# Layer norm of a convolution module: sums about the mean of six of eight feature tiles, made during the convolution's last groups, and two first maps of the second product in step

## The chip, the cores and the metric

The kernel runs on one core of one Trainium2 chip. The metric is the device time of one execution in microseconds; the time of a kernel is the median of its runs. The engines are named as in the profile: PE multiplies matrices (its weight loads are shown as PEld), DVE, ACT and POOL work on vectors, and DMA queues move data. Each engine takes its instructions in their order and stops at one whose operands or whose output buffer are not ready.

## What is computed

A trunk of two layers works on 1024 latent tokens and 256 context tokens of 1024 features. The first layer's mixer is a convolution module, the second's is attention; a feed-forward network (FFN) follows each. The change lies in the convolution module alone, between its convolution and its second product (`w_pw2`):

```python
def layernorm(x, g, b):
    xf = x.astype(jnp.float32)
    mu = jnp.mean(xf, axis=-1, keepdims=True)
    var = jnp.mean(jnp.square(xf - mu), axis=-1, keepdims=True)
    y = (xf - mu) * lax.rsqrt(var + EPS)
    return (y * g.astype(jnp.float32) + b.astype(jnp.float32)).astype(x.dtype)

def conv_module(h, w_pw1, b_pw1, w_dw, b_dw, ln_g, ln_b, w_pw2, b_pw2):
    u = h @ w_pw1 + b_pw1
    a, gt = jnp.split(u, 2, axis=-1)
    u = a * jax.nn.sigmoid(gt)
    u = lax.conv_general_dilated(u, w_dw[:, None, :].astype(u.dtype), ...) + b_dw
    u = jax.nn.silu(layernorm(u, ln_g, ln_b))
    return u @ w_pw2 + b_pw2
...
    yx = conv_module(hx, *cp)
    yc = conv_module(hc, *cp) if need_ctx else None
...
    x = x + g_x * rmsnorm(yx, norm_g[i, 1])
    ctx = ctx + g_c * rmsnorm(yc, norm_g[i, 1])
    fx = rmsnorm(x, norm_g[i, 2]) * (1.0 + scf_x) + shf_x
    x = x + gf_x * rmsnorm(swiglu(fx, ffn_w1[i], ffn_w3[i], ffn_w2[i]), norm_g[i, 3])
```

## The kernel before

**Layout.** Features lie on the 128 partitions, so 1024 features are eight feature tiles (KT = 8), and tokens run along the columns. Behind the convolution the tokens are three pieces: C (256 context tokens), L and R (512 latent tokens each).

**Convolution.** It has 64 groups: eight feature tiles of eight groups each (`conv`). A group is a run of matmuls (L497 and its neighbours) of weight maps, which DVE makes with one product each (L468), two for a group. The group's result in PSUM is drained by ACT with the bias (L498) into a buffer v, and DVE adds the second half to it (L500). In v the tokens of a feature tile stand in another layout, so a finished feature tile is stored to DRAM and loaded back token by token in order: `load_cv` (L537) brings it into the tensors of C, L and R (tags KB, T4, T5). The eighth tile of C goes from v to its tensor by eight DMAs, which ACT issues (L505). DVE sums each feature tile in v for the mean (`conv_sum`, L520 and L522), the eighth in two halves.

**Layer norm.** `ln` takes one piece: `mean` makes the mean of all its tokens on all partitions by matmuls with a constant (L530); for each of the eight tiles DVE subtracts it (L548), ACT squares (L351, L354) and DVE adds up (L355). `stat` sums over the partitions with matmuls of one column (L331), DVE scales them (L336) and takes the reciprocal root in eleven small operations (`rsqrt`, L309 to L317), and PE transposes it so that it stands on all partitions (L343). Then for each tile DVE multiplies by root and gain (L556), ACT does Silu with the bias (L558), and the result is split in a high half (ACT, L153) and a low half (DVE, L156).

**Products.** A product of float32 operands is three matmuls of such halves (`mm3`, L164 to L166: high by high, high by low, low by high). `pw2` makes eight maps of a piece, each of 8 x 3 matmuls over the eight tiles, with weights from `wload`: a DMA of 512 KB (L140), the high half on ACT (L141), the low half on DVE (L145). Two raw buffers (`wr`) and three buffers of each half (`wh`, `wl`) go round. ACT evacuates a map from PSUM (L572) and squares it for the sum that the RMS norm behind needs. `post_pre` does that norm, adds the residual (L592, L595), and makes the FFN's input (`apply`, L363 to L369).

**Order.** The program's text calls: normalise C, normalise L, maps of C, normalise R, maps of L, `post_pre` of C and L, maps of R, then the FFN of layer 0 over C and L, with R's `post_pre` beside it. A scheduler of the tile framework places instructions on each engine from that text by priorities (`later` puts an instruction further back). The first two weights of `pw2` are loaded during the convolution's last groups. PSUM has eight banks; the convolution goes round three (3, 4 and 7), maps and statistics have sets of banks that `set_banks` names.

## Time and profile before

| | |
|---|---|
| median of 3 runs | 3082.22 us (3081.51, 3082.22, 3088.68) |
| the profiled execution's own time | 3085.12 us |
| span of the profiled execution | 3083.3 us |
| busy in the span: PE | 2918.8 us (95%) |
| DVE | 1913.3 us (62%) |
| ACT | 1192.3 us (39%) |
| POOL | 259.8 us (8%) |

All durations below are of that one profiled execution. Times in the trace count from the span's start. The convolution ends near 392 us, the FFN's first matmul starts near 554 us; the stretch between them is the place of the change. A row of the trace shows the start, the busy time, the engine, the kernel's line, the operation, its output and its inputs with their shapes, the number of records in the row, and in brackets the idle time of the engine ahead of it with what ended that. PEclk is the clock that the chip granted to PE, as a share of full speed. Where a table row has a count but no time, it groups all instructions of one line.

### The profile page before, as it was taken

Reading aid. Unit: us, or ns where it says so; the run is one execution under the profiler, and the core shown is the slowest. Engines: PE = TensorE matmul, PEld = TensorE weight load, DVE = VectorE, ACT = ScalarE, POOL = GpSimd, SP = SyncE. Lnnn points to the kernel's source line nnn. Section 1 sums busy time; section 2 is a strip of 40 time slices with the busy share of each in tenths; the row PEclk is TensorE's granted clock in tenths of the full one; section 3 lists DMA queues with packets and bytes.
Section 4 is the critical chain, followed back from the end, with each engine's and each line's share of the span. In section 5 each row is a group of like instructions: output and inputs, shape, how many; then the busy total and the mean of one; then the engine's idle time right before and its main releaser. Section 6 shows DMA issues by size and latency. Waiting matters only on the chain. (4 is left out here: it accounts for less than half of the span.)

```text
span 3083.3 us, 38930 instructions
## 1 busy us (share of the span) xinstructions
PE 2918.8 (95%) x14974; PEld 2427.3 (79%) x14974; DVE 1913.3 (62%) x3355; ACT 1192.3 (39%) x1869; POOL 259.8 (8%) x413
## 2 busy tenths in 40 slices
PE   7999969998999999999988899979999999999997
PEld 5788858887888888888876678767777778788886
DVE  5886777897533257433574899776666653843335
ACT  5222255431211234222332688655555543332222
POOL 0000001123100011000013211110000000100000
PEclk9999979999999999999988999989999999999999
DMA  6542424466422234333355321222222232442232
GB/s 234 149 119 75 129 85 138 149 189 222 150 63 68 62 99 155 109 96 96 115 155 125 87 61 43 87 78 81 67 81 76 67 127 96 150 136 96 92 95 68
DMA packets 140714, 336.94 MB, mean 109 GB/s; under 512 B 39920, under 2 KB 61424, under 8 KB 139376
## 3 DMA queue, kind: packets, MB, share of 16 engines
q1 hardware_dynamic: 76432, 221.94, 22.3%
q0 software_dynamic: 37984, 104.42, 11.5%
q10 hardware_dynamic: 26112, 8.10, 1.1%
q8 instruction: 117, 1.92, 0.3%
q14 instruction: 69, 0.57, 0.1%
HBM read 289.76 MB, written 39.19 MB: 107 GB/s over the span
## 5 line engine op out<-in xcount | busy, mean ns | idle before, releaser
L164 PE MATMUL ps<-T,wh 128*128 128x512 f32 (+1 forms) x2256 | 852.9, 379 | 14.4 <-ACT T L153 5.5
L166 PE MATMUL ps<-T,wl 128*128 128x512 f32 (+1 forms) x2256 | 850.3, 378 | 15.6 <-DVE wl L145 15.6
L165 PE MATMUL ps<-T,wh 128*128 128x512 f32 (+1 forms) x2192 | 824.8, 377 | 1.0 <-DVE T L156 0.7
L141 ACT CAST wh<-wr 128x1024 fp32r<-128x1024 f32 x296 | 310.8, 1050 | 895.4 <-PE ps L165 672.5
L145 DVE TENSOR_TENSOR wl<-wr,wh 128x1024 fp32r<-128x1024 f32 x288 | 352.3, 1224 | 314.6 <-ACT wh L141 310.9
L166 PEld LDWEIGHTS ps<-T,wl 128*128 128x128 f32 x2256 | 431.8, 191 | 94.7 <-DVE wl L145 18.2
L164 PEld LDWEIGHTS ps<-T,wh 128*128 128x128 f32 x2256 | 431.4, 192 | 93.7 <-ACT T L153 7.0
L165 PEld LDWEIGHTS ps<-T,wh 128*128 128x128 f32 x2192 | 419.6, 191 | 74.8 <-DVE T L156 2.0
L165 PE MATMUL ps<-HS,wh 128*128 128x512 f32 (+1 forms) x784 | 304.2, 388 | 0.0
L853 DVE TENSOR_TENSOR T<-ps,T 128x512 fp32r<-128x512 f32 x320 | 216.9, 687 | 110.8 <-ACT T L852 109.7
L166 PE MATMUL ps<-HS,wl 128*128 128x512 f32 (+1 forms) x720 | 279.4, 388 | 0.0
L164 PE MATMUL ps<-HS,wh 128*128 128x512 f32 (+1 forms) x720 | 279.3, 390 | 0.0
L852 ACT CAST T<-ps 128x512 fp32r<-128x512 f32 x320 | 185.9, 585 | 191.7 <-PE ps L849 165.4
L849 PE MATMUL ps<-cst,T 128*128 128x128 f32 x1100 | 192.1, 276 | 15.5 <-DVE T L853 15.3
L681 DVE TENSOR_TENSOR T<-ps,T 128x512 f32<-128x512 f32 (+1 forms) x168 | 110.7, 664 | 146.3 <-PE ps L166 145.5
L837 DVE TENSOR_SCALAR_CACHE_REDUCE T<-ps,rq 128x1280 f32<-128x1280 f32 x110 | 170.0, 1545 | 42.0 <-PE ps L831 37.7
L849 PEld LDWEIGHTS ps<-cst,T 128*128 128x128 f32 x1100 | 133.5, 142 | 63.3 <-DVE T L853 43.5
L657 DVE TENSOR_TENSOR sm<-sm,ps 128x256 f32<-128x256 f32 (+1 forms) x88 | 54.6, 620 | 197.8 <-PE ps L166 197.8
L839 ACT ACTIVATE T<-T,mn 128x1280 f32<-128x1280 f32 x110 | 150.3, 1367 | 67.7 <-DVE T L837 65.8
L165 PEld LDWEIGHTS ps<-HS,wh 128*128 128x128 f32 x784 | 147.9, 189 | 28.8 <-DVE HS L156 0.2
L831 PE MATMUL ps<-KB,q 128*128 128x512 f32 (+1 forms) x576 | 143.5, 369 | 16.7 <-DVE T L837 8.2
L166 PEld LDWEIGHTS ps<-HS,wl 128*128 128x128 f32 x720 | 135.8, 189 | 27.0
(212 smaller groups left out, 4331.9 us busy)
## 6 DMA issues: line engine op xcount, KB each, us to landing
wr<-in_w SPq DMA_DIRECT2D x220, 512.0 KB, 3.5
q<-in_w SPq DMA_DIRECT2D x44, 512.0 KB, 3.5
wr<-in_pw SPq DMA_DIRECT2D x40, 512.0 KB, 3.6
q<-in_wmodT POOLq DMA_DIRECT2D x56, 256.0 KB, 3.4
HR<-in_wmodT POOLq DMA_DIRECT2D x56, 256.0 KB, 3.4
qsd<-T POOLq DMA_DIRECT2D x32, 256.0 KB, 10.9
q<-qsd POOLq DMA_DIRECT2D x32, 256.0 KB, 3.3
wr<-in_wo SPq DMA_DIRECT2D x16, 512.0 KB, 3.8
```

What stands on the lines that cost most here:

```text
L141: nc.scalar.copy(hi, raw)
L145: nc.vector.tensor_tensor(lo, raw, hi.bitcast(F32), op=ALU.subtract)
L164: nc.tensor.matmul(out[:, :n], lhsT=wh, rhs=xh, start=k == 0, stop=False)
L165: nc.tensor.matmul(out[:, :n], lhsT=wh, rhs=xl, start=False, stop=False)
L166: nc.tensor.matmul(out[:, :n], lhsT=wl, rhs=xh, start=False, stop=k == nk - 1)
L681: nc.vector.tensor_tensor(yd, out[:, :c1 - c0], yd, op=ALU.add)
L831: nc.tensor.matmul(sc[:, k0:k0 + w], lhsT=q[:, h, :], rhs=kt[:, p * TOK + k0:p * TOK + k0 + w], start=p == 0, stop=p == 1)
L837: nc.vector.tensor_scalar(out=pt, in0=sc, scalar1=rq[:, h:h + 1], scalar2=None, op0=ALU.mult, op1=ALU.min, accum_out=mn)
L839: nc.scalar.activation(pt, pt, AF.Exp, bias=mn, scale=-1.0, accum_out=sums[:, 0, h:h + 1])
L849: nc.tensor.transpose(tp[:, h * P:(h + 1) * P], Ps[h][:, j * P:(j + 1) * P], c["ident"])
L852: nc.scalar.copy(ph, tp)
L853: nc.vector.tensor_tensor(pl, tp, ph.bitcast(F32), op=ALU.subtract)
```

## The change

Normalising no longer starts from the mean of all eight feature tiles. `conv_sum` runs over the first six tiles only (KM = 6), and their mean, on three banks of its own for C, L and R (`ln_mean`), is subtracted as a shift. A variance about a shift needs two sums, of the values and of their squares: variance is the mean square less the square of the mean, both taken about the shift. `ln_tile` does for one tile and one piece the subtraction on DVE (now with a factor, so another form of operation), the square on ACT, and the sums over the partitions as one-column matmuls on PE (placed `later(100)`): for C both sums of each tile, for L and R the sum of the values of each tile, while their squares are added up on DVE as before and summed at the end. The first seven tiles of C and L are taken three at a time behind the convolution's groups from the seventh of the groups left in that loop on (`i > 5`); their eighth tiles and all of R stand behind the convolution.

`ln` then makes two numbers for each token, the reciprocal root and the mean by the root. Both are transposed to all partitions (two banks), and a tile is normalised by two operations of DVE (multiply, subtract) where there was one; the gain moves to the scale operand of ACT's Silu. In `pw2` the first two maps of each piece run in step (`projs`, `mm3s`): for each of the eight input tiles three matmuls of map 0 and three of map 1. The eight DMAs of C's eighth tile are issued by SP where ACT issued them. The banks are dealt out anew: sums of C and of R share bank 5, the maps have banks 7, 1, 6, the statistics behind them 3 and 4.

In the order of PE's instructions, the first place is behind the convolution's last group. In these rows `ps` is a PSUM bank, HS and T_2697 the convolution's data and maps, HR its sums, cst a constant, acc the summed squares, nr the reciprocal root, and T_3214 with wh the first map of C. Before:

```order
L497 MATMUL ps<-HS,T_2697 128x324
L530 MATMUL ps<-HR,cst 128x32 x8
L331 MATMUL ps<-cst,acc 128x1 x2
L343 MATMUL ps<-cst,nr 128x128 x2
L164 MATMUL ps<-T_3214,wh 128x256 x3
L165 MATMUL ps<-T_3214,wh 128x256
```

In the changed kernel PE has these rows there; KB, T_3011 and T_3019 are the tensors of C, L and R, sb the squares of a C tile, ne the mean by the root, and L176 is a product of C:

```order
L515 MATMUL ps<-HS,T_2697 128x324
L567 MATMUL ps<-cst,KB 128x1 x2
L567 MATMUL ps<-cst,sb 128x1 x2
...
L567 MATMUL ps<-cst,T_3011 128x1 x28
L567 MATMUL ps<-cst,KB 128x1 x2
L567 MATMUL ps<-cst,sb 128x1 x2
L567 MATMUL ps<-cst,T_3019 128x1 x28
L596 MATMUL ps<-cst,nr 128x128 x2
L567 MATMUL ps<-cst,T_3011 128x1 x4
L596 MATMUL ps<-cst,ne 128x128 x2
L567 MATMUL ps<-cst,T_3019 128x1 x4
L567 MATMUL ps<-cst,acc 128x1 x4
L176 MATMUL ps<-T_3310,wh 128x256 x2
```

Sums of L and of seven tiles of R now stand on PE between C's sums and C's transposes, and the eighth tiles' sums between the transposes and C's first product.

The second place is on DVE, where R is normalised beside the first maps of L. HS is R's normalised low half, T_3655 or T_3774 its high half, `wr` and `wl` the raw and low half of a weight. Before, the splits of the weights of maps 0 to 3 of L stand further ahead, and that of map 4 is the one in these rows:

```order
L556 SCALAR_TENSOR_TENSOR T_3022<-T_3022,cst,ps 128x512 x5
L156 TENSOR_TENSOR HS<-T_3022,T_3655 128x512 x2
...
L556 SCALAR_TENSOR_TENSOR T_3022<-T_3022,cst,ps 128x512
L156 TENSOR_TENSOR HS<-T_3022,T_3655 128x512 x2
L145 TENSOR_TENSOR wl<-wr_74,wh 128x1024
L156 TENSOR_TENSOR HS<-T_3022,T_3655 128x512 x2
```

In the changed kernel it is the split of map 3 of L, and it is behind 23 of the 24 operations of R:

```order
L602 TENSOR_TENSOR T_3019<-T_3019,ps 128x512 x2
L603 TENSOR_TENSOR T_3019<-T_3019,ps 128x512 x2
...
L603 TENSOR_TENSOR T_3019<-T_3019,ps 128x512
L157 TENSOR_TENSOR HS<-T_3019,T_3774 128x512
L373 TENSOR_TENSOR acc<-acc,sb 128x512
L146 TENSOR_TENSOR wl<-wr_73,wh 128x1024
L157 TENSOR_TENSOR HS<-T_3019,T_3774 128x512
```

The split of a weight has moved back by one map against the normalisation of R. The same holds, still on DVE, beside the last maps of R, where L's residual is added (L592 and L595 before, L642 and L645 after; T_3689 and T_3816 are L's tensor, HR the residual). Before, the split ahead of that is that of R's map 6:

```order
L145 TENSOR_TENSOR wl<-wr_74,wh 128x1024
L592 SCALAR_TENSOR_TENSOR T_3689<-T_3689,col_2944,ps 128x512 x2
L595 TENSOR_TENSOR T_3689<-T_3689,HR 128x512 x2
...
L595 TENSOR_TENSOR T_3689<-T_3689,HR 128x512 x2
L145 TENSOR_TENSOR wl<-wr_73,wh 128x1024
```

In the changed kernel the split of map 6 stands behind all sixteen operations:

```order
L642 SCALAR_TENSOR_TENSOR T_3816<-T_3816,col_2944,ps 128x512 x2
L645 TENSOR_TENSOR T_3816<-T_3816,HR 128x512 x2
...
L645 TENSOR_TENSOR T_3816<-T_3816,HR 128x512 x2
L146 TENSOR_TENSOR wl<-wr_74,wh 128x1024
```

The split for map 6 has gone from the row ahead of L's residual to the row behind it, where map 7's was. The diff:

```diff
--- before.py
+++ after.py
@@ -38,6 +38,7 @@
 NM = 5
 CG = 8
 NC_, NL = CTX // PH, SEQ // PH
+KM = KT - 2
 UW = 2 + NC_ + 2 + NL + 2
 OW = UW - 4
 PIECES = {"C": (0, CTX), "L": (CTX, CTX + 512), "R": (CTX + 512, TOK)}
@@ -164,6 +165,23 @@
             nc.tensor.matmul(out[:, :n], lhsT=wh, rhs=xh, start=k == 0, stop=False)
             nc.tensor.matmul(out[:, :n], lhsT=wh, rhs=xl, start=False, stop=False)
             nc.tensor.matmul(out[:, :n], lhsT=wl, rhs=xh, start=False, stop=k == nk - 1)
+
+    def mm3s(self, outs, ws, x, nk, n):
+
+        nc = self.nc
+        for k in range(nk):
+            xh, xl = x(k)
+            for out, w in zip(outs, ws):
+                wh, wl = w(k)
+                nc.tensor.matmul(out[:, :n], lhsT=wh, rhs=xh, start=k == 0, stop=False)
+                nc.tensor.matmul(out[:, :n], lhsT=wh, rhs=xl, start=False, stop=False)
+                nc.tensor.matmul(out[:, :n], lhsT=wl, rhs=xh, start=False, stop=k == nk - 1)
+
+    def projs(self, outs, waps, x, n):
+        def cols(w):
+            return lambda k: (w[0][:, k * P:(k + 1) * P], w[1][:, k * P:(k + 1) * P])
+        ws = [cols(self.pre.pop(0) if self.pre else self.wload(w)) for w in waps]
+        self.mm3s(outs, ws, x, KT, n)
 
     def proj(self, out, wap, x, n):
         hi, lo = self.pre.pop(0) if self.pre else self.wload(wap)
@@ -502,16 +520,15 @@
                 for d, o0, nn in ((self.vc, 0, NC_), (self.vl, 2 + NC_, NL)):
                     if k == KT - 1 and d is self.vc:
                         for j in range(CG):
-                            nc.scalar.dma_start(self.cvs["C"][16 * j:16 * j + 16, k, :], v[:, j, :NC_])
+                            nc.sync.dma_start(self.cvs["C"][16 * j:16 * j + 16, k, :], v[:, j, :NC_])
                     else:
                         nc.scalar.dma_start(d[k].rearrange("g q n -> q g n"), v[:, :, o0:o0 + nn])
                 if k == KT - 1:
                     self.load_cv("L", k)
                     self.load_cv("R", k)
 
-                self.conv_sum(v[:, CG // 2:] if k == KT - 1 else v, k)
-            elif k == KT - 1 and g == CG // 2 - 1:
-                self.conv_sum(v[:, :CG // 2], k)
+                if k < KM:
+                    self.conv_sum(v, k)
             yield
 
     def conv_sum(self, v, k):
@@ -521,41 +538,70 @@
         if k:
             nc.vector.tensor_tensor(self.vsum, self.vsum, r, op=ALU.add)
 
-    def mean(self, b):
-
-        nc = self.nc
-        ps = self.bank("st")
+    def ln_mean(self, b, ps):
+
+        nc = self.nc
         nn, o, s0 = {"C": (NC_, 0, 0), "L": (NL, 2 + NC_, 0), "R": (NL, 2 + NC_, 4)}[b]
         for i in range(PH if b == "C" else 4):
             nc.tensor.matmul(ps[:, i * nn:(i + 1) * nn], lhsT=self.c["selp"][:, s0 + i:s0 + i + 1].to_broadcast([P, P]),
                              rhs=self.vsum[:, o:o + nn], start=True, stop=True)
-        return ps
+
+    def ln_tile(self, b, k, mean, sums):
+
+        nc = self.nc
+        n = PIECES[b][1] - PIECES[b][0]
+        x, J = self.cvs[b][:, k, :], n // P
+        nc.vector.scalar_tensor_tensor(out=x, in0=mean[:, :n], scalar=-float(KT) / KM, in1=x, op0=ALU.mult, op1=ALU.add)
+        if b == "C":
+            sq = self.sb(n)
+            nc.scalar.activation(sq, x, AF.Square)
+            vs = (x, sq)
+        else:
+            if k == 0:
+                self.lnacc[b] = self.acc(n)
+            self.sq_acc(self.lnacc[b], x, k)
+            vs = (x, self.lnacc[b]) if k == KT - 1 else (x,)
+        with self.later(100):
+            for i, v in enumerate(vs):
+                for j in range(J):
+                    nc.tensor.matmul(sums[:, i * J + j:i * J + j + 1], lhsT=v[:, j * P:(j + 1) * P], rhs=self.c["ones"],
+                                     start=k + i + j == 0, stop=k == KT - 1 and i == 1 and j == J - 1)
 
     def load_cv(self, b, k):
         d = (self.vc if b == "C" else self.vl)[k].rearrange("g (c s) n -> (g c) (s n)", s=PH)
         n = PIECES[b][1] - PIECES[b][0]
         self.nc.sync.dma_start(self.cvs[b][:, k, :], d[:, 512:] if b == "R" else d[:, :n])
 
-    def ln(self, b, stags, box):
+    def ln(self, b, stags, box, mean, sums, bcast):
 
         nc, c = self.nc, self.c
         c0, c1 = PIECES[b]
         n = c1 - c0
+        J = n // P
         cv = self.cvs[b]
-        mean = self.mean(b)[:, :n]
-        acc = self.acc(n)
-        for k in range(KT):
-            nc.vector.tensor_tensor(cv[:, k, :], cv[:, k, :], mean, op=ALU.subtract)
-            self.sq_acc(acc, cv[:, k, :], k)
+        for k in range(KT if b == "R" else 0):
+            self.ln_tile(b, k, mean, sums)
             yield
-        pb = self.stat(acc, n)
+
+        m, q, e = (self.tiny([P, 16], t) for t in ("nv", "nd", "ne"))
+        d, v = m[:, :J], m[:, J:2 * J]
+        nc.vector.tensor_scalar(out=m[:, :2 * J], in0=sums[:, :2 * J], scalar1=1.0 / D, scalar2=None, op0=ALU.mult)
+        nc.vector.tensor_tensor(q[:, :J], d, d, op=ALU.mult)
+        nc.vector.scalar_tensor_tensor(out=v, in0=v, scalar=EPS, in1=q[:, :J], op0=ALU.add, op1=ALU.subtract)
+        r = self.rsqrt(v, J)
+        nc.vector.tensor_tensor(e[:, :J], d, r, op=ALU.mult)
+        for ps, t in zip(bcast, (r, e)):
+            for j in range(J):
+                with self.later(16):
+                    nc.tensor.transpose(ps[:, j * P:(j + 1) * P], t[:, j:j + 1].to_broadcast([P, P]), c["ident"])
+        pr, pd = (ps[:, :n] for ps in bcast)
         shi, slo = self.halves(*stags, n)
         box.append((shi, slo))
         for k in range(KT):
             z = cv[:, k, :]
-            nc.vector.scalar_tensor_tensor(out=z, in0=z, scalar=c["lng"][:, k:k + 1], in1=pb,
-                                           op0=ALU.mult, op1=ALU.mult)
-            nc.scalar.activation(z, z, AF.Silu, bias=c["lnb"][:, k:k + 1], scale=1.0)
+            nc.vector.tensor_tensor(z, z, pr, op=ALU.mult)
+            nc.vector.tensor_tensor(z, z, pd, op=ALU.subtract)
+            nc.scalar.activation(z, z, AF.Silu, bias=c["lnb"][:, k:k + 1], scale=c["lng"][:, k:k + 1])
             self.split(shi[:, k, :], slo[:, k, :], z)
             yield
 
@@ -567,8 +613,12 @@
         yacc = self.acc(n)
         box.append((y, yacc))
         for k in range(KT):
-            o = self.bank("mm")
-            self.proj(o, self.a["pw2"][k], self.pairs(*s), n)
+            if k == 0:
+                os = [self.bank("mm") for _ in range(2)]
+                self.projs(os, self.a["pw2"][0:2], self.pairs(*s), n)
+            o = os[k] if k < 2 else self.bank("mm")
+            if k > 1:
+                self.proj(o, self.a["pw2"][k], self.pairs(*s), n)
             nc.scalar.activation(y[:, k, :], o[:, :n], AF.Identity, bias=c["bpw2"][:, k:k + 1], scale=1.0)
             self.sq_acc(yacc, y[:, k, :], k)
             yield 24 * n / 2400
@@ -998,23 +1048,37 @@
         for g0 in (0, CG // 2):
             self.split_u(KT - 1, g0, g0 + CG // 2)
         self.derive(0, (1, 2))
+        bk = [self.ps[:, i, :] for i in range(8)]
+        shift = {"C": bk[0], "L": bk[1], "R": bk[2]}
+        sums = {"C": bk[5], "L": bk[6], "R": bk[5]}
+        bcast = {"C": (bk[0][:, :CTX], bk[0][:, CTX:]), "L": (bk[3], bk[4]), "R": (bk[2], bk[0])}
+        self.lnacc = {}
+        early = [(b, k) for b in ("C", "L") for k in range(KT - 1)]
         for i, _ in enumerate(cg):
             if i in (2, 4):
                 self.pre.append(self.wload(a["pw2"][i // 2 - 1]))
-        self.set_banks(mm=[0, 1, 2, 3, 4, 7], st=[5, 6])
+            if i == 5:
+                for b in PIECES:
+                    self.ln_mean(b, shift[b])
+            for _ in range(3 if i > 5 else 0):
+                if early:
+                    b, k = early.pop(0)
+                    self.ln_tile(b, k, shift[b], sums[b])
         sv, yv, fv = ({b: [] for b in PIECES} for _ in range(3))
         tags = {"C": ("KB", ("T1", "T1"), ("T1", "T1")), "L": ("T4", ("T2", "T3"), ("T2", "T3")),
                 "R": ("T5", ("T6", "HS"), ("T4", "T6"))}
 
         def pp(b):
             return self.post_pre(0, *yv[b][0], a["xT"], self.x1d, *PIECES[b], 0, "HR", tags[b][2], fv[b])
+        self.set_banks(mm=[7, 1, 6], st=[3, 4])
         for b in ("C", "L"):
-            for _ in self.ln(b, tags[b][1], sv[b]):
+            self.ln_tile(b, KT - 1, shift[b], sums[b])
+        for b in ("C", "L"):
+            for _ in self.ln(b, tags[b][1], sv[b], shift[b], sums[b], bcast[b]):
                 pass
-            self.bank("st")
         for _ in self.pw2("C", tags["C"][0], sv["C"][0], yv["C"]):
             pass
-        for _ in self.ln("R", tags["R"][1], sv["R"]):
+        for _ in self.ln("R", tags["R"][1], sv["R"], shift["R"], sums["R"], bcast["R"]):
             pass
         for _ in self.pw2("L", tags["L"][0], sv["L"][0], yv["L"]):
             pass
```

## The prediction

> **What bounds the kernel now.** I read the windows of the convolution's end first, then the rows of PE, DVE and ACT there. C, L and R are the three token pieces (256, 512, 512 columns); m0 to m7, L0 to L7 and R0 to R7 are their eight maps of the second product.
>
> ```profile
> core 0: us, PE busy (x) PEld busy (x) DVE busy (x) ACT busy (x) POOL busy (x), PEclk, DMA share, GB/s
> 391.00:410.00 19.00, 5.72 (x25) 4.87 (x24) 11.38 (x37) 6.44 (x15) 0.00 (x0) 0.57 0.19 58
> 430.00:444.80 14.80, 7.80 (x55) 7.11 (x53) 13.51 (x27) 12.71 (x23) 0.00 (x0) 0.77 0.23 73
> 457.30:482.00 24.70, 24.70 (x105) 20.41 (x106) 20.71 (x39) 15.81 (x26) 0.00 (x0) 0.91 0.28 88
> 482.00:504.00 22.00, 22.00 (x102) 18.26 (x100) 10.10 (x11) 11.56 (x17) 0.00 (x0) 1.00 0.43 141
> ```
>
> Between the convolution and L0, PE is mostly idle and DVE or ACT is late; from 457.3 us PE is full. So an edit ahead of 457 us is worth what it does to the start of that full stretch, and a hole made in the stretch costs its full length. The last row holds L4 to L7: 22.0 / 4 = 5.5 us a map, 0.227 us a matmul. PE's rows with their waits:
>
> ```profile
> 379.79 0.34 PE L497 MATMUL ps<-HS,T 128*128 128x324 f32 x1
> ...
> 389.62 0.35 PE L497 MATMUL ps<-HS,T 128*128 128x324 f32 x1
> ...
> 390.92 0.35 PE L497 MATMUL ps<-HS,T 128*128 128x324 f32 x1
> 394.75 3.62 PE L530 MATMUL ps<-HR,cst 128*128 128x32 f32 x16 [3.48 <-DVE HR L522]
> 403.94 1.02 PE L331 MATMUL ps<-cst,acc 128*128 128x1 f32 x4 [5.57 <-DVE acc L355]
> 407.38 0.69 PE L343 MATMUL ps<-cst,nr 128*128 128x128 f32 x2 [2.42 <-DVE nr L317]
> 409.87 1.01 PE L164 MATMUL ps<-T,wh 128*128 128x256 f32 x3 [1.81 <-ACT T L153]
> ...
> 416.16 0.28 PE L165 MATMUL ps<-T,wh 128*128 128x256 f32 x1
> 416.28 0.28 PE L166 MATMUL ps<-T,wl 128*128 128x256 f32 x1
> ...
> 426.70 0.95 PE L331 MATMUL ps<-cst,acc 128*128 128x1 f32 x8
> ...
> 442.47 2.08 PE L530 MATMUL ps<-HR,cst 128*128 128x128 f32 x8 [6.75 <-DVE T L556]
> ...
> 454.09 0.50 PE L164 MATMUL ps<-T,wh 128*128 128x512 f32 x1 [1.52 <-ACT wh L141]
> ...
> 457.29 0.80 PE L166 MATMUL ps<-T,wl 128*128 128x512 f32 x1 [2.47 <-DVE wl L145]
> ...
> 547.88 0.50 PE L166 MATMUL ps<-T,wl 128*128 128x512 f32 x1 [1.29 <-DVE wl L145]
> ...
> 562.21 1.01 PE L164 MATMUL ps<-T,wh 128*128 128x512 f32 x2 [4.00 <-ACT T L368]
> ```
>
> C's statistics (two sums, two transposes) cost PE little, and its first map starts at 409.87. A C matmul takes 0.12 us (416.16 to 416.28, 2.9 us a map). Two later stops carry my argument: at 457.29 PE waits for the low half of L0's weights, split on DVE; at 562.21 it waits for L's input to the FFN. DVE's rows:
>
> ```profile
> 378.19 0.32 DVE L500 TENSOR_TENSOR HR<-HR,ps 128x162 f32<-128x162 f32 x1
> 378.43 0.82 DVE L468 TENSOR_TENSOR T<-q,cst 128x640 fp32r<-128x640 f32 x1
> 379.16 2.49 DVE L520 TENSOR_REDUCE sm<-HR 128x162 f32<-128x1296 f32 x1
> ...
> 398.41 1.42 DVE L548 TENSOR_TENSOR KB<-KB,ps 128x256 f32<-128x256 f32 x4 [3.71 <-PE ps L530]
> ...
> 433.26 2.06 DVE L556 SCALAR_TENSOR_TENSOR T<-T,cst,ps 128x512 f32<-128x512 f32 x3
> ...
> 443.53 1.22 DVE L145 TENSOR_TENSOR wl<-wr,wh 128x1024 fp32r<-128x1024 f32 x1
> ...
> 446.74 3.08 DVE L548 TENSOR_TENSOR T<-T,ps 128x512 f32<-128x512 f32 x5
> ...
> 456.02 1.22 DVE L145 TENSOR_TENSOR wl<-wr,wh 128x1024 fp32r<-128x1024 f32 x1
> ...
> 470.47 3.38 DVE L556 SCALAR_TENSOR_TENSOR T<-T,cst,ps 128x512 f32<-128x512 f32 x5 [1.21 <-PE ps L343]
> ...
> 479.51 1.22 DVE L145 TENSOR_TENSOR wl<-wr,wh 128x1024 fp32r<-128x1024 f32 x1
> ...
> 559.52 1.23 DVE L145 TENSOR_TENSOR wl<-wr,wh 128x1024 fp32r<-128x1024 f32 x1 [4.64 <-ACT wh L141]
> 560.66 2.06 DVE L363 SCALAR_TENSOR_TENSOR sb<-T,col,ps 128x512 f32<-128x512 f32 x3
> ```
>
> DVE takes its queue in order, so a split behind a normalisation waits for it: m6's (443.53) behind L's, which began at 433.26; L4's (479.51) inside R's (from 470.47), where it hurt nothing because L1 to L3 were split already. From these rows, a two-input operation costs 0.60 us at 512 columns (3.08 for five) and 0.34 at 256 (1.42 for four), a drain of a convolution group 0.24 and a map product 0.73 (378.19 to 379.16). A split takes 1.22, 1.13 before the next operation can follow. PE's rows give the reciprocal root: 2.4 from the sums' end at 404.96 to the transposes at 407.38.
>
> **The change, step by step.**
>
> *Convolution's end.* The reduction of the seventh tile (2.49) and the two halves of the eighth, as wide together, leave DVE: with three adds, some 5.8 us. In their place, ahead of the last five drains, stand seven subtractions each of C, L and R: 7 x 0.34 + 14 x 0.60 = 10.8 us. Their form has no row of that kind here; the nearest are L651 (below: constant scalar, 0.68 us) and L556 (column scalar, 2.06 for three). So 0.60 to 0.66 each; I take 0.60, by the constant scalar. The three means (32 records) run on PE behind the group that ended at 380.1 (379.79), 3.9 us at full clock; then five groups of 1.30 (389.62 to 390.92), with 24 records of sums between them, end at 393.5. DVE: five map products and three drains from 378.43 end at 382.8; 10.8 us of subtractions and five drains more, at 394.8, against 393.05. Eight DMAs leave ACT for SP. They made ACT's step:
>
> ```profile
> 390.91 0.40 ACT L498 ACTIVATE HR<-ps,cst 128x162 f32<-128x162 f32 x1 [0.99 <-DVE HR L500]
> 391.70 0.55 ACTq L505 DMA_DIRECT2D KB<-HR  x1
> 392.30 0.40 ACT L498 ACTIVATE HR<-ps,cst 128x162 f32<-128x162 f32 x1 [0.99 <-DVE HR L500]
> ...
> 435.89 1.33 ACT L558 ACTIVATE T<-T,cst 128x512 f32<-128x512 f32 x2
> 437.13 1.12 ACT L153 CAST T<-T 128x512 fp32r<-128x512 f32 x2
> ...
> 454.76 2.69 ACT L354 ACTIVATE sb<-T 128x512 f32<-128x512 f32 x5
> L651 DVE SCALAR_TENSOR_TENSOR sm<-sm,ps 128x512 f32<-128x512 f32 x22 | 14.9, 680 | 0.0
> wr<-in_pw SPq DMA_DIRECT2D x40, 512.0 KB, 3.6
> ```
>
> That step (1.39 us a group, 390.91 to 392.30) goes, but DVE is now the late one, so I count nothing for it. On SP only loads that wait for the same drains stand behind them.
>
> *One-column sums.* Before, C, L and R need 10 such matmuls, now 104, each of two records with a weight load apiece. Eight records took 0.95 us at full clock (426.70), 0.12 each; four took 1.02 at the low clock (403.94), 0.25 each. PE has just run the convolution, so I take 0.12. The order shows that L's 28 do not lie beside the convolution: they and four more C tiles stand behind its last group (393.5): 32 records to 397.3, L's 56 to 404.0, C's last 8 to 405.0. R's 56 use C's bank, so they wait until DVE has read it (405.2) and end at 412.0; only then come C's transposes, though the root is ready at 407.6. Before: 407.38.
>
> Then DVE's second entry is L's statistic, which waits for 24 more records and ne's transposes (415.6). C's first normalised tile is done at 416.3, its first product at 417.9, **8 us later** than 409.87.
>
> The Trainium skill, "TensorE: Matmul & The Clock Gate", Part 1, says that about 3.4 us of sustained activity gives the full clock and an idle window of that length takes it back. By it the sums run at full clock behind the convolution, and the sum below stays +10.5. Part 4 of that page says that transposes do not count as busy in the same way; if that held of one-column work too, the sum would be +23. Here 16 small records in 3.62 us (394.75) did not raise the clock, and no row has a long run of them at full clock, so the trace settles neither.
>
> *C and L normalised.* The factor moves to ACT's operand for nothing; DVE takes two operations where one was: C costs 24 x 0.34 + 2 of roots = 10 us, from 415.7 to 425.8. m0 to m2 have weights and end at 430.2. m3's split stands behind 22 of L's 24 operations, 13.2 us from 426.3, and 0.7 of waiting for ACT, which has two weight casts and two evacuations first: 440.2, done 441.4. Before, m6 was at that point at 444.75. What hid the change's gain: R's mean no longer stops PE (6.75 us at 442.47), but the same L operations now hold m3. Five maps at 2.9, with about 2 us lost to the low clock after the idle, end at 457.6. So L0's third matmul comes at 458.0, against 457.29: **+0.8**.
>
> *L in step, R's normalisation.* L0 and L1 together take 48 x 0.227 = 10.9, with R's sums and eight transposes 13.3, to 470.9. Three weight buffers exist, and L2's split is done (464). L3's stands in DVE's queue behind R's normalisation, which can begin only after those transposes (469.7). It comes after 23 operations of 0.60 and an add, 14.4 us, and ACT, with L3's and L4's casts and the evacuations first and 1.13 a tile (0.62 + 0.51, above), stretches it to 485.6. PE has L2 alone to hide it, and arrives at 476.8: **idle 8.8 us**. It resumes at the low clock, as at 457.29: there the window of 24.7 us had 0.91 of the clock, 9% or 2.2 us lost. I add 2.2. L3 ends at 493.1; before at 482, where the window of L4 begins. **+11**.
>
> *To the FFN.* L4 to L7 have their splits in time: 514.9. R0 and R1 take 10.9, R2 to R5 5.5 each, sums and transposes 2.7: 550.5. R6's split stands behind L's post (from 541.2; 8 x 0.66 + 14 x 0.60 = 13.7 us), so R6 waits from 551.0 to 556.1 and is slow again; before, R7 lost 1.29 there. R6 ends at 563.2. L's second statistic stands behind nine matmuls of R7 (2.0); its sums take 1.0, the root with a split in it 3.3, transposes 0.4: L's input starts on DVE at 569.9, against 560.66: **+9.2**. In exchange, the split that stood ahead of that (559.52, after 4.64 idle) now stands behind it, for the product that follows: +1 to +2. The rest of the program has the same order, and the FFN is full of PE.
>
> **Sum: +10.5 us.** The profiled run took 3085.1 us (span 3083.3, 1.8 around it), 2.9 above the median 3082.2. So 3095.6 against itself, 3092.7 against the median.
>
> Bounds: a first part 5 us quicker or R6's wait gone gives +5; both, +0.5. Subtractions at 0.66 add 0.8; a weight load that lands in 6 instead of 3.6 us adds up to 2; sums at 0.25 add 12 to 14, that is +23.
>
> **Rivals.**
>
> *The lateness is absorbed (not slower).* PE's end before was loose by 4.0 at 562.21 and 1.29 at 547.88. If R's normalisation hides behind L2 because ACT's casts come earlier, and R6 behind R5, only the first part counts: +0.8 less those 5.3, so -4.5, about 3078. It decides when L3's and R6's waits together stay under 5.3 us. For it: DVE was only 10.1 of 22 us busy at 482 to 504. Against it: both splits stand in order behind work that begins too late, 14.4 and 13.7 us for 5.5 of cover.
>
> *Sums at the low clock.* Some 100 of the records between 393.5 and 415 at 0.25 instead of 0.12 move C's start by 12 to 13 us, and all behind it: 3105. For it: 394.75, where the clock stayed low. Against it: 426.70, eight such records at full clock amid other work.
>
> *The early work comes through (faster).* If the sums run between convolution groups in spite of their order, C starts at 410 as before, 8 us earlier than in my sum, and with both waits hidden as in the first rival that gives 0.8 - 8 - 5.3 = -12.5: 3070. Against it is the order, which an engine does not pass.
>
> **How the numbers follow.** My forecast (+4 to +16 us, 3086 to 3098) has 0.6, absorbed 0.23, low clock 0.1, faster 0.07. The range, 3077 to 3103, leaves out the last two and little of the others. A measurement tells 0.3% (9.2 us) from no change. Of the forecast's 0.6, 0.38 lies above that bound: with the low clock 0.48 slower. Its other 0.22 and 0.21 of the absorbed case are within: 0.43. The rest, 0.02 and 0.07, is faster: 0.09.
>
> **What would show it.** Right: C's transposes about 412; the first product about 418; a wait of PE for a DVE split of 8 to 9 us near 477 and of about 5 near 551; the FFN's L part some 9 to 12 us late. Wrong: C's product before 413, sums at 0.25, or no stop of PE between L0 and L7.

## The result, and the profile after

The changed kernel takes 3118.01 us (median of 4 runs, 3113.43 to 3127.42) and the kernel before, in its four runs beside it, 3085.45 us (3081.51 to 3093.88). The ratio is 1.0099, with a 95% interval of 1.0078 to 1.0121: it is slower by about 1%, 30 us, three times the forecast and outside its range. The profiled execution took 3118.28 us (span 3116.5), 33.2 us more than that of before.

The windows of the changed kernel at the convolution's end, in the columns that were used above (PE, PEld, DVE, ACT, POOL, then PEclk):

```profile
380.00:388.00 8.00, 8.00 (x68) 8.00 (x67) 8.00 (x19) 3.49 (x10) 1.24 (x2) 1.00 0.77 224
388.00:392.00 4.00, 4.00 (x37) 4.00 (x35) 4.00 (x9) 1.23 (x3) 0.00 (x0) 1.00 0.11 18
392.00:400.00 8.00, 8.00 (x39) 8.00 (x39) 4.73 (x9) 2.70 (x5) 0.00 (x0) 0.50 0.03 4
400.00:426.00 26.00, 25.75 (x122) 25.66 (x122) 6.59 (x23) 4.00 (x6) 2.83 (x4) 0.50 0.26 82
426.00:434.00 8.00, 5.88 (x29) 5.80 (x29) 2.50 (x10) 1.36 (x3) 0.00 (x0) 0.50 0.00 0
```

PE is busy almost without a pause from 380 to 426 us, and yet the granted clock falls to 0.50 at 392 and stays there up to 434. What it is busy with, from the timeline of PE with its waits:

```profile
379.89 3.73 PE L546 MATMUL ps<-HR,cst 128*128 128x32 f32 x32
...
388.70 0.50 PE L567 MATMUL ps<-cst,KB 128*128 128x1 f32 x4
...
399.97 12.09 PE L567 MATMUL ps<-cst,T 128*128 128x1 f32 x56
...
414.02 12.11 PE L567 MATMUL ps<-cst,T 128*128 128x1 f32 x56 [0.25 <-DVE nv L588]
425.99 0.67 PE L596 MATMUL ps<-cst,nr 128*128 128x128 f32 x2
...
434.18 0.80 PE L176 MATMUL ps<-T,wh 128*128 128x256 f32 x2 [2.30 <-ACT T L154]
...
458.72 0.58 PE L167 MATMUL ps<-T,wl 128*128 128x256 f32 x1 [11.35 <-DVE wl L146]
...
503.38 0.79 PE L167 MATMUL ps<-T,wl 128*128 128x512 f32 x1 [7.96 <-DVE wl L146]
...
576.14 0.67 PE L167 MATMUL ps<-T,wl 128*128 128x512 f32 x1 [4.67 <-DVE wl L146]
```

The one-column sums are L567. At first four records take 0.50 us (388.70), 0.12 each, later 56 take 12.1, 0.21 each. C's first product starts at 434.18 us, where it was 409.87 before. Behind it stand the three waits for a weight's low half that the prediction named: m3's (458.72), L3's (503.38) and R6's (576.14). On DVE, L3's split and L's input to the FFN:

```profile
501.51 0.68 DVE L373 TENSOR_TENSOR acc<-acc,sb 128x512 f32<-128x512 f32 x1
502.11 1.22 DVE L146 TENSOR_TENSOR wl<-wr,wh 128x1024 fp32r<-128x1024 f32 x1
...
585.51 2.06 DVE L381 SCALAR_TENSOR_TENSOR sb<-T,col,ps 128x512 f32<-128x512 f32 x3 [1.77 <-PE ps L361]
```

### The profile page after: what moved, and what is told of

Read it like the earlier page. It is cut to its first block, busy times and chain, and to the rows that moved or that the text cites. A ratio compares the mean times of both kernels' runs of the same rounds, so it can differ in the third digit from the quotient of the medians.

```text
span 3116.5 us, 39346 instructions
## 1 busy us (share of the span) xinstructions
PE 2954.4 (95%) x15172; PEld 2466.2 (79%) x15172; DVE 1918.9 (62%) x3375; ACT 1196.7 (38%) x1869; POOL 260.3 (8%) x413
## 3 DMA queue, kind: packets, MB, share of 16 engines
q10 hardware_dynamic: 24960, 7.96, 1.1%
## 5 line engine op out<-in xcount | busy, mean ns | idle before, releaser
L167 PE MATMUL ps<-T,wl 128*128 128x512 f32 (+1 forms) x2208 | 832.6, 378 | 33.6 <-DVE wl L146 33.6
L165 PE MATMUL ps<-T,wh 128*128 128x512 f32 (+1 forms) x2208 | 835.1, 379 | 6.7 <-ACT T L154 3.9
L166 PE MATMUL ps<-T,wh 128*128 128x512 f32 (+1 forms) x2160 | 812.3, 376 | 0.6 <-DVE T L387 0.4
L167 PEld LDWEIGHTS ps<-T,wl 128*128 128x128 f32 x2208 | 422.0, 191 | 110.3 <-DVE wl L146 35.6
L165 PEld LDWEIGHTS ps<-T,wh 128*128 128x128 f32 x2208 | 422.2, 191 | 83.1 <-ACT T L154 5.0
L166 PEld LDWEIGHTS ps<-T,wh 128*128 128x128 f32 x2160 | 412.3, 191 | 72.8 <-DVE T L157 1.2
```

The lines of the kernel that those rows point to most:

```text
L165: nc.tensor.matmul(out[:, :n], lhsT=wh, rhs=xh, start=k == 0, stop=False)
L166: nc.tensor.matmul(out[:, :n], lhsT=wh, rhs=xl, start=False, stop=False)
L167: nc.tensor.matmul(out[:, :n], lhsT=wl, rhs=xh, start=False, stop=k == nk - 1)
```

## The experiments

Times moved a little from one set of runs to the next (the kernel before had medians of 3085.45 to 3088.98), so each kernel is compared by its ratio to the kernel before in the same set; 0.001 is 3.1 us, and what a version gains or loses is worked out from the ratios. The changed kernel's own ratio is 1.0099.

### Are the sums slow because they move one column?

Each sum is made with 32 equal columns, same weights, same count:

```diff
-nc.tensor.matmul(sums[:, i * J + j:i * J + j + 1], lhsT=v[:, j * P:(j + 1) * P], rhs=self.c["ones"],
+o = (i * J + j) * 32
+nc.tensor.matmul(sums[:, o:o + 32], lhsT=v[:, j * P:(j + 1) * P], rhs=self.c["ones"].to_broadcast([P, 32]),
...
-in0=sums[:, :2 * J]
+in0=sums[:, :2 * J * 32].rearrange("p (a w) -> p a w", w=32)[:, :, 0]
```

> The changed kernel, with each one-column sum (128x1) made as the same matmul with 32 equal columns (128x32), so the same weights and the same count of records. Theory clock: a long run of one-column matmuls does not hold PE's clock, and the trace's 0.50 of the clock from 400 to 434 us comes from them; the means with 32 columns (3.73 us for 32 records, at 379.89) ran at the full clock, so 32 columns hold it. Then a record takes 0.12 and not 0.21 us, C's first product comes near 418 to 420 instead of 434.18 us, and the time falls by 13 to 17 us, to 3101 to 3105. Theory other cause: the clock falls there whatever the sums do (the end of the convolution alone, or the weight load of each record). Then the records stay at 0.21 us, the clock at 0.50 to 0.55 from 400 to 426 us, and the time stays at 3115 to 3121.

Measured: 1.0098 (1.0076 to 1.0119), the time of the other cause. The clock did not hold. But it fell at 395.2 us, later than with one column, and with one column it had fallen at 392.0, ahead of the convolution's last matmul (392.94): both speak against the convolution's end as the cause. (The 391.2 in the next expectation is too early; from 391 to 392 us the clock of the changed kernel was still 0.99.) So the same edit was run with 64 columns:

> The changed kernel with 64 equal columns in each sum (32 columns did not hold the clock: it fell at 395.2 us, four microseconds later than with one column, 391.2). Theory columns: what holds the clock is how many columns stream in a given time; 64 columns stream twice as many, so the clock falls later still or not at all, and C's first product comes at 418 to 427 us; the time is 3102 to 3112. Rival, the convolution's end: the clock falls 3 to 4 us after the last convolution matmul whatever small matmuls follow; then it falls at 395 to 397 us, C's first product comes at 430 us and the time is as with 32 columns, 3114 to 3120.

Measured: 1.0031 (1.0021 to 1.0040), 21 us less than the changed kernel, and less than the first theory had named. Windows with 32 columns, then with 64:

```profile
392.00:396.00 4.00, 4.00 (x35) 4.00 (x34) 3.74 (x8) 2.36 (x5) 0.00 (x0) 0.90 0.05 8
396.00:426.00 30.00, 29.75 (x141) 29.61 (x141) 7.33 (x25) 4.00 (x6) 2.84 (x4) 0.50 0.22 71
```

```profile
392.00:400.00 8.00, 8.00 (x73) 8.00 (x73) 6.76 (x13) 4.68 (x9) 0.70 (x1) 1.00 0.30 77
400.00:414.00 14.00, 13.12 (x116) 12.85 (x116) 7.24 (x30) 3.78 (x7) 2.13 (x4) 1.00 0.32 110
```

PE's timeline with 64 columns (the sums are L568 here):

```profile
396.01 6.42 PE L568 MATMUL ps<-cst,T 128*128 128x64 f32 x56
...
407.65 0.38 PE L597 MATMUL ps<-cst,nr 128*128 128x128 f32 x2
...
413.68 0.50 PE L176 MATMUL ps<-T,wh 128*128 128x256 f32 x2 [0.62 <-ACT T L154]
...
440.54 0.58 PE L167 MATMUL ps<-T,wl 128*128 128x256 f32 x1 [6.28 <-DVE wl L146]
...
482.93 0.79 PE L167 MATMUL ps<-T,wl 128*128 128x512 f32 x1 [8.11 <-DVE wl L146]
...
554.07 0.79 PE L167 MATMUL ps<-T,wl 128*128 128x512 f32 x1 [4.39 <-DVE wl L146]
```

With 64 columns the clock stays at 1.00 through all the sums. It falls behind C's first product, from 415.1 to 418.5 us, where PE has had short waits. The 56 sums that took 12.09 us with one column take 6.42, 0.11 us a record, though each moves 64 times as many columns. So it is the count of columns that decides, not the end of the convolution, nor that PE is busy: with 1, 32 and 64 columns PE is equally busy, and during the sums the clock falls at about 392, at about 395, and not at all. What exactly the chip counts, and where between 32 and 64 the border lies, these runs don't say. The clock's changes in the trace of one execution are whole multiples of 3.41 us apart (in the changed kernel 391.98, 439.77, 450.01 and 463.66 us: 14, 3 and 4 of them), so a fall that is 3 us later is about one such step later.

### Are the sums too many?

The shift is the mean of tiles 0 to 5, so the sum of all values of these tiles about it is zero but for rounding. Only tiles 6 and 7 are summed:

```diff
-vs = (x, sq)
+vs = (x if k >= KM else None, sq)
...
-vs = (x, self.lnacc[b]) if k == KT - 1 else (x,)
+vs = (x if k >= KM else None, self.lnacc[b] if k == KT - 1 else None)
```

> The changed kernel without the sums of the values over tiles 0 to 5, which are zero about the mean of just these tiles: 44 one-column matmuls in place of 104, 24 fewer each for L and R and 12 for C. Theory clock and count: behind the convolution's end stand about 48 matmuls (96 records) fewer at 0.21 us, 20 us, of which DVE's own queue (the last additions of squares, done near 403 us in the changed kernel) gives back some; C's first product near 414 to 418 us, the time 3098 to 3102. Theory engine DVE: what holds C's start is DVE (drains and subtractions, then the reciprocal root), and PE's sums lie beside it; then the first product comes no earlier than 428 us and the time stays above 3112.

Measured: 1.0029 (1.0018 to 1.0040), 3098.4 us, as the first theory had it; C's first product came at 411.99 us, 2 us before the 414 to 418 that were expected. PE's rows:

```profile
390.42 1.84 PE L567 MATMUL ps<-cst,sb 128*128 128x1 f32 x16
...
394.35 0.58 PE L567 MATMUL ps<-cst,sb 128*128 128x1 f32 x4
398.66 1.01 PE L567 MATMUL ps<-cst,KB 128*128 128x1 f32 x4 [3.72 <-DVE KB L554]
...
411.99 0.80 PE L176 MATMUL ps<-T,wh 128*128 128x256 f32 x2 [2.30 <-ACT T L154]
```

Forty one-column records, from 390.42 to 394.93, still ran at the full clock here. The sums behind them run at the low clock from 398.66 us on, where PE had waited 3.72 us for C's eighth tile. So the one-column sums can be repaired in two ways, fewer or wider, and both give back some 21 us of 30 us. What is left, 9 to 10 us, is about the size of the forecast.

### The two maps in step

Taken out of the changed kernel (`projs` undone in `pw2`), and put alone into the kernel before:

```diff
-            if k == 0:
-                os = [self.bank("mm") for _ in range(2)]
-                self.projs(os, self.a["pw2"][0:2], self.pairs(*s), n)
-            o = os[k] if k < 2 else self.bank("mm")
-            if k > 1:
-                self.proj(o, self.a["pw2"][k], self.pairs(*s), n)
+            o = self.bank("mm")
+            self.proj(o, self.a["pw2"][k], self.pairs(*s), n)
```

> The changed kernel with the maps of the second product one after another, as before the change. Theory order: the waits for the low halves of the weights of m3 (11.35 us), L3 (7.96) and R6 (4.67) come from the splits' place in DVE's queue behind a normalisation, and not from the step of two maps; each piece has the same 192 products, and the time stays within 4 us of 3118. Rival: two maps in step use up two weights at once and move each later split back; without it the waits at L3 and R6 go, and the time falls by 8 to 12 us, to 3106 to 3110.

Measured: 1.0097 (1.0077 to 1.0117), no change.

> The kernel before with one part of the change alone: the first two maps of each piece in step. Theory order: the splits keep their places ahead of R's normalisation and of L's residual, so the time stays within 4 us of the kernel before (3081 to 3089). Rival: the step of two maps alone moves a split behind a normalisation; then PE stops 5 to 11 us for a low half near 470 to 480 us or 548 us, and the time is 3090 to 3096.

Measured: 1.0031 (1.0019 to 1.0043), slower by 9.6 us, where within 4 was expected. The waits of the rival are there, though shorter than its 5 to 11 us. PE's waits without the step in the changed kernel, then with the step alone in the kernel before:

```profile
504.47 0.80 PE L167 MATMUL ps<-T,wl 128*128 128x512 f32 x1 [5.81 <-DVE wl L146]
...
567.02 0.79 PE L167 MATMUL ps<-T,wl 128*128 128x512 f32 x1 [7.18 <-DVE wl L146]
```

```profile
481.06 0.79 PE L166 MATMUL ps<-T,wl 128*128 128x512 f32 x1 [2.73 <-DVE wl L145]
...
538.98 0.65 PE L360 MATMUL ps<-cst,nr 128*128 128x128 f32 x4 [2.41 <-DVE sb L380]
554.75 0.50 PE L166 MATMUL ps<-T,wl 128*128 128x512 f32 x1 [4.39 <-DVE wl L145]
```

The same kinds of wait stand in both: for a low half of L's weights and for one of R's. The reading that fits is that either part of the change is enough to move the splits behind the work of DVE, and that undoing one of the two therefore gives nothing back; it is argued from these rows and not shown. The step's cost was then tried with just those two splits on POOL:

> The kernel before with two maps in step, and the low halves of L's map 3 and R's map 6 on POOL. With two maps in step alone the time was 0.31% above before (9.6 us), with waits of 2.74 us for L3's half at 481 and 4.39 us for R6's at 555. Theory order: the step costs only by those two splits' new places; with both on POOL the time is within 3 us of the kernel before (ratio 0.999 to 1.001). Rival: the step costs by itself (both maps' weights, or PSUM banks held longer): the ratio stays at 1.002 to 1.004.

Measured: 1.0051 (1.0036 to 1.0065), not better. The wait at 481 is gone, and others have come:

```profile
485.47 0.43 PE L362 MATMUL ps<-cst,nr 128*128 128x128 f32 x2 [3.38 <-DVE nr L336]
...
542.68 0.79 PE L168 MATMUL ps<-T,wl 128*128 128x512 f32 x1 [6.89 <-DVE wl L147]
```

The waits are others, for other work, so the order of the stretch is not the old one less two splits. So this run does not tell the step's own cost from the cost of the order; that stays open.

### The splits on POOL

```diff
+LOP = {'C': (2, 3, 4, 5, 6, 7), 'L': (3, 4), 'R': (6, 7)}
...
+self.lo_dve = 0.0 if k in LOP[b] else 1.0
 self.proj(o, self.a["pw2"][k], self.pairs(*s), n)
+self.lo_dve = 1.0
```

> The changed kernel, with the low halves of some weights of the second product split on POOL (2.4 us each in the trace, row of POOL) and not on DVE: maps 2 to 7 of C, 3 and 4 of L, 6 and 7 of R. Theory order: the waits of PE near 447 (11.35 us), 495 (7.96) and 571 us (4.67) come from these splits' place in DVE's queue behind the normalisations of L and R and L's residual; off that queue they shrink to 0 to 3 us each, and the time falls by 14 to 22 us, to 3096 to 3104. Rival: the high halves on ACT stand behind Silu in the same way, or the two raw buffers come free no earlier; then each wait stays above half its length and the time above 3108.

Measured: 1.0056 (1.0041 to 1.0071), 13 us less than the changed kernel, just short of the 14 to 22 that were expected; the median, 3109.51 us, lies above the 3108 that the rival named. PE's rows, those of POOL near the third of them, then a step of R's root on DVE in the changed kernel, and the same root here:

```profile
453.93 0.39 PE L166 MATMUL ps<-T,wh 128*128 128x256 f32 x1 [3.40 <-ACT wh L143]
456.36 0.58 PE L168 MATMUL ps<-T,wl 128*128 128x256 f32 x1 [1.93 <-POOL wl L149]
...
486.87 1.12 PE L597 MATMUL ps<-cst,nr 128*128 128x128 f32 x4 [4.28 <-DVE nr L336]
```

```profile
480.25 2.39 POOL L149 TENSOR_TENSOR wl<-wr,wh 128x1024 fp32r<-128x1024 f32 x1 [14.91 <-ACT wh L143]
483.25 2.36 POOL L149 TENSOR_TENSOR wl<-wr,wh 128x1024 fp32r<-128x1024 f32 x1 [0.61 <-ACT wh L143]
```

```profile
484.74 0.17 DVE L327 TENSOR_SCALAR nq<-nv 128x4 int32<-128x4 int32 x1
```

```profile
480.36 2.31 DVE L328 TENSOR_SCALAR nq<-nv 128x4 int32<-128x4 int32 x1
483.32 2.38 DVE L336 SCALAR_TENSOR_TENSOR nr<-nq,nr 128x4 f32<-128x4 f32 x2
```

m3's wait of 11.35 us has become 3.40 + 1.93, partly the rival's wait for the high half on ACT; L3's of 7.96 and R6's of 4.67 are gone. A new one of 4.28 us, for R's reciprocal root, goes with POOL's splits: the root's first step, 4 columns wide, takes 2.31 us where it took 0.17, and two later ones 2.38; both rows end, within 0.1 us, where POOL's splits end (482.64 and 485.61). Not every operation of DVE is held up in this way. Two of the same run, beside two splits of POOL:

```profile
453.96 5.15 POOL L149 TENSOR_TENSOR wl<-wr,wh 128x1024 fp32r<-128x1024 f32 x2 [7.39 <-ACT wh L143]
```

```profile
454.43 2.43 DVE L158 TENSOR_TENSOR T<-T,T 128x512 fp32r<-128x512 f32 x1
456.79 0.68 DVE L604 TENSOR_TENSOR T<-T,ps 128x512 f32<-128x512 f32 x1
```

L158 reads no operand from PSUM and takes 2.43 us, where it takes 0.68 without POOL; L604 reads one from PSUM (`ps`) and keeps its 0.68. The control is the kernel before with nine of its splits on POOL (the same edit, maps 3 to 7 of C, 0 and 4 of L, 6 and 7 of R):

> The kernel before with low halves of weights of the second product on POOL: maps 3 to 7 of C, 0 and 4 of L, 6 and 7 of R. It tells whether POOL's splits are worth something without the change. In the trace of before only 2.47 us at L0 and 1.29 us at R7 are waits for such a half, so at most 4 us come back, and a split takes 1.2 us longer on POOL: within 4 us of the kernel before. Rival: DVE's queue, shorter by nine splits of 1.2 us, brings L's and R's normalisations forward, and the time falls by 6 to 12 us.

Measured: 0.9988 (0.9974 to 1.0003), no change that the runs can tell, as expected.

### Both repairs, and all three

> Both edits to the changed kernel: the sums of the values over tiles 6 and 7 alone (the others are zero about their mean), and the same splits on POOL. Theory (the change's loss is the one-column sums on PE plus the splits behind the normalisations, which add): 20 us from the first edit and 14 to 22 from the second, so 3076 to 3084, faster than the kernel before in the same call by 5 to 12 us. Rival (the two hide each other: with C earlier, DVE's normalisations are the bound whoever splits): 3088 to 3098.

Measured: 0.9986 (0.9974 to 0.9999), 4 us below the kernel before by the ratio (1.7 us by the medians, 3087.25 and 3088.98): 1 us short of the 5 to 12 us that the first theory gave against before. The two edits add: the splits on POOL are worth 0.0043 (13 us) here as in the changed kernel (1.0029 to 0.9986, and 1.0099 to 1.0056). R's root falls on POOL's splits here too: PE waits 4.18 us for it at 466.51.

> Three edits to the changed kernel: sums of the values over tiles 6 and 7 alone, 64 equal columns in each sum, and the splits on POOL. The second run with these but one column (sums of two tiles, splits on POOL) had C's first product at 411.07 us and the clock at 0.50 from 398 to 412. Theory: with the clock held, the sums between 398 and 410 us halve and the first maps start warm; the first product comes at 405 to 408 us, and the time is 4 to 8 us less than that run, 7 to 13 us below the kernel before (ratio 0.996 to 0.998). Rival: the first maps then wait for the high half of m2's weights on ACT (3.41 us at 433.66 there) and L's normalisation instead, and the ratio stays at 0.998 to 1.000.

Measured: 0.9961 (0.9946 to 0.9976), 3073.98 us against 3087.73 for the kernel before: 12 us faster by the ratio. The size is the expected one, but not for the expected reason. Its PE rows:

```profile
397.45 1.12 PE L569 MATMUL ps<-cst,KB 128*128 128x64 f32 x4 [3.75 <-DVE KB L555]
...
410.27 0.79 PE L177 MATMUL ps<-T,wh 128*128 128x256 f32 x2 [1.51 <-ACT T L155]
...
457.45 0.65 PE L598 MATMUL ps<-cst,nr 128*128 128x128 f32 x4 [0.23 <-DVE nr L336]
```

With so few sums PE now waits 3.75 us for C's eighth tile, and behind that wait the sums start at the low clock (0.50 from 397 to 412 us) whatever their width; C's first product comes at 410.27, not at the 405 to 408 that were expected and hardly earlier than with one column (411.07). About half of the gain of 8 us over that run is at 457.45: in this order R's root is done before POOL's next split begins (457.92), and the wait of 4.18 us is 0.23. Some 2 us had been gained by C's third map, whose wait for its high half ends at 431.46 in place of 433.66; the rest was not taken apart.

> As the run before it in this call, with the maps of the second product one after another. Theory (two maps in step cost nothing when the splits that they push back are on POOL): the same within 3 us. Rival (the step alone costs, as it did by 0.31% in the kernel before): 5 to 10 us less.

Measured: 0.9962 (0.9947 to 0.9977), the same: in this version the step costs nothing that the runs can tell.

> As the run before it in this call, and R's mean is made behind C's normalisation, in C's bank, so that R's subtractions and sums no longer stand on DVE and PE ahead of C's statistics. Theory (R's early work holds C back): C's transposes 2 to 4 us earlier and C's first product at 401 to 405 us, while R's mean and sums stop PE later as before the change (6.75 us there), so the net is between 3 us gained and 4 us lost. Rival: C's start is held by its own eighth tile and by DVE's drains; then C's start does not move, and only the loss is seen, 4 to 8 us.

```diff
-shift = {"C": bk[0], "L": bk[1], "R": bk[2]}
+shift = {"C": bk[0], "L": bk[1], "R": bk[0]}
...
-                for b in PIECES:
+                for b in ("C", "L"):
...
+        self.ln_mean("R", shift["R"])
```

Measured: 0.9958 (0.9944 to 0.9972), the same within the interval. C's first product comes at 407.25, 4.3 us earlier than in the run that it alters (411.53), though not at the 401 to 405 that were expected. Of the 4.3 us, 2.5 are left at R's transposes (460.58 against 463.07), and in the time nothing shows clearly. The first theory's price, a stop of PE for R's mean, did not come: that mean (425.78) stands without a wait. These last three beat both kernels and can't be told from one another.

## Why the prediction was wrong

**The step that failed** is "PE has just run the convolution, so I take 0.12" a record, in the part on one-column sums, and the sentence behind it in the sum: C's start at 417.9 us. PE went from the convolution into 176 records of one column almost without a pause, 24 such records ran among the convolution's last matmuls, and the clock fell at 392 us. The 176 took about 0.213 us each (56 from 414.02 to 425.99), so 176 x 0.093 = 16.4 us more than at 0.12. C's first product came at 434.18 instead of 417.9: 16.3 us late. With 64 columns, that is with the clock held, it came at 413.68, 4.2 us ahead of the forecast; about half of this is an order that differs a little (36 of R's records stand ahead of C's transposes, not 56).

**The rival had the right mechanism and a wrong size.** "Sums at the low clock" was given 12 to 13 us, a time of 3105 and a chance of 0.1. The sum counted "some 100 of the records"; the same working had listed 32 + 56 + 8 + 56 + 24 = 176. And its chance was too low: 394.75 of before, 16 small records that did not raise the clock, was the nearest row, and eight such records amid other work (426.70) say nothing of a long run of them. The Trainium skill, "TensorE: Matmul & The Clock Gate", Part 1, ties the full clock to sustained activity; taken as PE's busy time, the trace disagrees, with 0.50 of the clock in 26 us that were busy for 25.75. Part 4 of the same page of the Trainium skill says of transposes that they don't count as busy in the same way; the runs show the like of one-column products, and none of them tests transposes. That the width decides is from the runs alone.

**What behind it held.** The steps, in us of the trace, with the idle times of PE:

| step | forecast | changed kernel | with 64 columns |
|---|---|---|---|
| C's transposes | 412.0 | 425.99 | 407.65 |
| C's first product | 417.9 | 434.18 | 413.68 |
| PE goes on behind m3's wait | 441.4 | 458.72 | 440.54 |
| idle for L3's low half | 8.8 | 7.96 | 8.11 |
| idle for R6's low half | 5.1 | 4.67 | 4.39 |
| L's input to the FFN, on DVE | 569.9 | 585.51 | 563.81 |
| ratio to before | 1.0034 | 1.0099 | 1.0031 |

Less the 16.3 us, m3's wait ends 1.0 us from where it was forecast, and the two later waits end within 4 us of their places and are within 1 us of their sizes: the order of the splits against the normalisations was read rightly, from the order of instructions and the rows of before.

That the total fits too, +10.5 us forecast and 9.6 with the clock held, is in part luck. With 64 columns L's input to the FFN came 3.15 us later than before (560.66), where 9.2 were forecast: C's first product was 4.2 us early, and from the end of R6's wait to that input 9.7 us passed (554.07 to 563.81), not 13.8 (556.1 to 569.9). So most of the loss lies behind that input, where 1 to 2 us were forecast. In the changed kernel the input came 24.85 us later than before, and 9.2 + 16.3 is 25.5; there R6's wait ended 3.7 us later than forecast, and the 9.4 us behind it, again not 13.8, made up for it.

**The other rivals.** The lateness was not absorbed: with the clock held, both waits are there in full. The early work did not come through: C's product never came at 410 in the changed kernel, though it came near that, at 411.99, 410.27 and 407.25, in versions with fewer sums.

**What was not seen.** The step of two maps was counted as a part of one sum. Alone in the kernel before it costs 9.6 us, as much as the whole forecast, and its removal from the changed kernel gives nothing, as if the two parts of the change shared one loss; how they do is not shown. Of the 33.2 us between the two profiled executions the first-product term (16.3) and the forecast's 10.5 make 26.8; the other 6 lie behind L's input to the FFN (8.3 us were lost there) and were not taken apart.

## What to carry to other kernels

Before narrow matmuls are moved into a gap of PE, look not only whether PE is free but what they do to the clock of what runs beside and behind them: a long run of one-column products cost this kernel 16 us at a place where PE showed almost no idle time, and the same products with 64 equal columns took half as long. First leave out sums that are known in advance (here, of values about their own mean). And where two edits may each push the same instruction back in the same queue, undoing one can show nothing: test each alone on the kernel before, too.

## What the runs showed of the hardware

- PE busy 25.75 of 26 us and the clock at 0.50 (one column); the same records with 64 columns at 1.00. A record of 64 columns took 0.11 us, one of one column 0.21.
- In the convolution's last 32-column run ahead of that (379.89, 32 records in 3.73 us) the clock did not fall; with 32 columns for all sums it fell at about 395.2, 7 us after the first of them (388.12), convolution matmuls among them. In another run forty one-column records, 4.5 us from 390.42 on, ran at the full clock. How long a run is harmless is not settled here.
- While POOL split a weight (2.39 us), an operation of DVE on 4 columns took 2.31 us in place of 0.17 and ended with it: moving work to an idle POOL is not free for DVE. An operation of 512 columns with both operands outside PSUM took 2.43 us beside such splits in place of 0.68, and one with an operand in PSUM kept its 0.68.
